# FoX attention head loop on one core: a finished pair's division and splits, the next pair's transposes, the rows of maxima and the probability copies

## The chip, the cores and the metric

One core of a Trainium2 chip runs the whole layer. The metric is device time in microseconds for one execution, as the median over several executions. TensorE (PE, with its weight loads as PEld), VectorE (DVE), ScalarE (ACT) and GpSimd (POOL) each work through their instructions in order; all DMAs of this kernel are issued from SyncE (SP), also in order.

## The reference

One encoder layer over 1024 frames of width 1024: a forgetting-attention group of 8 heads of 64 and an RG-LRU group, mixed by `w_out`, then a SwiGLU block. What the change touches is the attention:

```python
s = jnp.einsum('bhqd,bhkd->bhqk', qb, kb).astype(jnp.float32) * scale
s = s + (cum_logf[:, :, start:end, None] - cum_logf[:, :, None, :end])
s = jnp.where(mask[None, None], s, -jnp.inf)
p = jax.nn.softmax(s, axis=-1).astype(vb.dtype)
outs.append(jnp.einsum('bhqk,bhkd->bhqd', p, vb))
...
mixed = jnp.concatenate([rmsnorm(att, attn_out_g[l]), rmsnorm(rec, lru_out_g[l])], axis=-1)
x = x + mixed @ w_out[l]
```

All numbers are float32. The kernel keeps float32 accuracy on TensorE by splitting an operand into a rounded part and a rest (`split`: the rounded part is made on ACT, the rest on DVE), so that one product becomes three matmuls.

## The kernel before, in words

The heads are taken one after the other, `h` = 0 to 7; two heads make a pair `p`. A head has 12 steps (`att_steps`): four key blocks for the first half of the queries (512 of them), eight for the second half. A step makes scores transposed, keys by queries, in a PSUM bank `st` (3 of them): L676 multiplies one split part, L677 adds the rest together with two extra rows, the bias of the key and the row of maxima of the query, and L679 adds the causal mask on the diagonal. ACT takes the exponential into `pt` (L684, 3 buffers). The rounded copy `ringh` is made on ACT (L686) or on DVE (L688), in turn, the rest `ringl` on DVE (L689), in a ring of four. LAG[h] steps later PE multiplies them with the values into bank `o` (L698, three matmuls). Row 64 of the values is ones, so the denominators come out with the outputs; ACT copies both out (`oe`, L704), and SP takes them to `attr` and `dq`.

The row of maxima of a head is found one head ahead (`max_steps`): for each of eight query blocks `qb` PE makes plain scores in a bank `mx` (2 of them, L284, L286), DVE takes the maximum (L287, `nm`); `rows(half)` transposes four columns of them (`mt`, L296, also in an `mx` bank), ACT copies the row (`mr`, L298), and a DMA puts it into the score operands (`set`, L299). Before, `rows(0)` comes after block 3 and `rows(1)` after block 7.

Between the steps of a head other work is interleaved, a list `extra` of pieces at a pace set by RATE[h]: at even heads `prep` (the transposes of the next pair's q and k, L250, and their split into `kh`, `kl`, `qh`, `ql`), the DMAs of `load_max`, the eight `max_steps`, `vprep` (values of the next head: cast on ACT, rest on POOL, L650), and at heads 2, 4 and 6 `finish_pair` of the pair before it: `spread` takes reciprocals of the denominators on DVE (L731) and sends them through DRAM (`rd`) to a tile `rb` (L732, L735), POOL multiplies the whole `attr` by it (L719, 128x1024), then come the split (L75 on ACT, L76 on DVE), the square on ACT and the sum of squares on POOL (L725). At head 7 `finish_6` does the same for head 6, with L740 on POOL, and `load_wa` brings the eight pieces of `w_out` for the attention half, through two buffers. Besides, 32 units of the LRU half's output projection (`fl`, L783, 12 matmuls each, in the single bank `tr`, evicted on DVE at L785) fill the steps at a pace FILL[h].

The code is written in that order, and a scheduler of the tile framework orders each engine's instructions from it when the kernel is built, from its own estimates of durations. So a piece can land some instructions away from where it is written.

## Time and profile before

| | us |
|---|---|
| median of 3 runs | 1193.15 |
| lowest, highest | 1187.73, 1193.55 |
| the profiled execution, its time | 1189.54 |
| its span, first to last instruction | 1187.8 |
| its mean granted TensorE clock | 0.991 |
| attention loop in the trace, from the first L676 to the last L698 | 268 to 462 |

The profiled execution lies between the lowest and the median run. The loop that the change touches is a sixth of the span. In the rows further down, a busy time is the time in which the engine had work, an idle time carries the name of the instruction that ended it, and DVE also counts as busy while one of its instructions is held up inside its own duration.

### The profile page before, as it was taken

The numbers are of one execution on the slowest core, as the hardware profiler recorded it, in microseconds if no ns is written. First come the engines' busy times: TensorE is split into PE (matmuls) and PEld (weight loads), VectorE is DVE, ScalarE is ACT, GpSimd is POOL, SyncE is SP. The second block draws the span as 40 slices with busy tenths as digits, with TensorE's granted clock in tenths as the row PEclk, the third lists the DMA queues.
The fourth block names the chain that finished last, engine by engine and source line by source line (L and its number), as shares of the span: only waits on it lengthen the run. The fifth ranks groups of instructions, "written<-read, shape, count | busy, mean of one in ns | idle before, by whom it ended". The sixth has DMA issues, their size and how long they took to land.

```text
span 1187.8 us, 16586 instructions
## 1 busy us (share of the span) xinstructions
PE 1146.5 (97%) x6137; PEld 971.1 (82%) x6137; DVE 812.5 (68%) x1357; ACT 514.6 (43%) x931; POOL 228.4 (19%) x192
## 2 busy tenths in 40 slices
PE   8999999998999899999699898999999999999998
PEld 7988999996878777788478787888888888888887
DVE  6436858768787866776768766865545555769693
ACT  7427766326555554433233233333333334444442
POOL 1000010012010211027433333442424200000000
PEclk9999999999999999999889999999999999999999
DMA  6021111135665667540455646333122489842220
GB/s 249 19 55 52 38 37 37 30 72 126 169 151 144 165 161 207 168 153 21 169 201 205 255 164 237 133 114 107 54 89 73 140 289 340 289 154 98 92 86 36
DMA packets 94924, 159.71 MB, mean 134 GB/s; under 512 B 13105, under 2 KB 56217, under 8 KB 93434
## 3 DMA queue, kind: packets, MB, share of 16 engines
q1 hardware_dynamic: 94842, 158.65, 42.3%
q8 instruction: 48, 0.79, 0.3%
q14 instruction: 34, 0.28, 0.1%
HBM read 103.41 MB, written 38.63 MB: 120 GB/s over the span
## 4 chain that ended last, share of the span: by engine, by line
PE 70%; DVE 14%; DMA 9%; issue 3%; ACT 2%; POOL 1%; SPq 1%; DVEq 0%; POOLq 0%; ACTq 0%
PE P L1371 17%; PE Pu L936 10%; PE Pg L936 8%; DMA wd<-in_w_down_dram 4%; PE pag L361 4%; PE pbk L377 4%; PE pbv L377 4%; PE pax L361 4%; PE pbq L377 3%; PE o L698 3%; PE fl L783 3%; DVE wd L1025 3%; DMA td<-wd 2%; PE mx L284 1%; PE st L676 1%
## 5 line engine op out<-in xcount | busy, mean ns | idle before, releaser
L1118 ACT ACTIVATE g<-g 128x512 f32<-128x512 f32 x40 | 25.3, 632 | 106.1 <-DVE g L1117 105.7
L684 ACT ACTIVATE pt<-st 128x512 f32<-128x512 f32 (+1 forms) x96 | 47.9, 508 | 53.5 <-PE st L679 26.5
L1025 DVE TENSOR_TENSOR wd<-wd 128x512 f32<-128x512 f32 x44 | 43.6, 992 | 39.7 <-DMA wd<-in_w_down_dram 39.1
L689 DVE TENSOR_TENSOR ringl<-pt,ringh 128x512 fp32r<-128x512 f32 (+2 forms) x96 | 57.7, 615 | 7.2 <-ACT ringh L686 5.8
L287 DVE TENSOR_REDUCE nm<-mx 128x1 f32<-128x512 f32 (+2 forms) x96 | 51.2, 550 | 11.1 <-PE mx L286 6.9
L783 PE MATMUL fl<-worec,rech 128*128 128x256 f32 x256 | 53.3, 290 | 0.9 <-DVE ql L76 0.7
L783 PEld LDWEIGHTS fl<-worec,rech 128*128 128x128 f32 x256 | 42.6, 193 | 3.1 <-DVE ql L76 1.1
L1117 DVE TENSOR_TENSOR g<-pug,Pg 128x512 f32<-128x512 f32 x30 | 20.5, 684 | 27.4 <-PE Pg L936 18.8
L676 PE MATMUL st<-set 128*128 128x512 f32 (+1 forms) x96 | 35.5, 372 | 3.3 <-ACT pt L684 3.2
L698 PE MATMUL o<-ringh,vh 128*128 128x512 f32 (+1 forms) x96 | 37.8, 394 | 0.0
L698 PE MATMUL o<-ringl,vh 128*128 128x512 f32 (+1 forms) x96 | 35.0, 365 | 2.1 <-DVE ringl L689 2.1
L783 PE MATMUL fl<-worec,recl 128*128 128x256 f32 x128 | 36.5, 285 | 0.0
L480 POOL TENSOR_TENSOR sqR<-sqR,i 128x1024 f32<-128x1024 f32 x3 | 7.2, 2397 | 150.8 <-ACT i L479 150.8
L1115 DVE TENSOR_TENSOR g<-g,puu 128x512 f32<-128x512 f32 x40 | 35.2, 879 | 0.3
L698 PE MATMUL o<-ringh,vl 128*128 128x512 f32 (+1 forms) x96 | 34.3, 358 | 0.3 <-POOL vl L650 0.3
L650 POOL TENSOR_TENSOR vl<-vn,vh 128x256 fp32r<-128x256 f32 x16 | 12.3, 776 | 112.1 <-ACT vh L649 112.1
L1114 DVE TENSOR_TENSOR puu<-puu,Pu 128x512 f32<-128x512 f32 x30 | 20.4, 682 | 17.9 <-PE Pu L936 17.8
L1086 POOL TENSOR_TENSOR S1g<-graw,graw 128x512 f32<-128x512 f32 x10 | 14.6, 1463 | 80.2 <-DVE au12l L73 12.5
L435 DVE SCALAR_TENSOR_TENSOR xc<-xr,vcol,xc 128x1023 f32<-128x1023 f32 (+2 forms) x12 | 15.4, 1280 | 18.5 <-ACT xc L433 18.4
L686 ACT CAST ringh<-pt 128x512 fp32r<-128x512 f32 (+1 forms) x48 | 26.4, 549 | 1.6 <-PE o L698 0.8
L861 PE MATMUL wa<-wah,atth 128*128 128x512 f32 x64 | 26.0, 406 | 1.0 <-ACT wah L72 1.0
L1086 POOL TENSOR_TENSOR S1u<-uraw,uraw 128x512 f32<-128x512 f32 x10 | 12.9, 1287 | 72.6 <-DVE ag92l L73 9.3
(2185 smaller groups left out, 4081.2 us busy)
## 6 DMA issues: line engine op xcount, KB each, us to landing
graw<-in_w_gate_dram SPq DMA_DIRECT2D x22, 512.0 KB
uraw<-in_w_up_dram SPq DMA_DIRECT2D x22, 512.0 KB
wd<-in_w_down_dram SPq DMA_DIRECT2D x22, 512.0 KB
gd<-g SPq DMA_DIRECT2D x22, 512.0 KB
td<-wd SPq DMA_DIRECT2D x11, 1024.0 KB
xt<-in_x_dram SPq DMA_DIRECT2D x8, 512.0 KB
set<-qh SPq DMA_DIRECT2D x16, 256.0 KB
xp<-in_x_dram SPq DMA_DIRECT2D x32, 128.0 KB
```

What stands on the lines that cost most here:

```text
L287: dve.tensor_reduce(out=nm[:, ch * 8 + qb:ch * 8 + qb + 1], in_=ps[:, :nk], axis=AX.X, op=ALU.max, negate=True)
L361: pe.matmul(ps[g][:, :n], a, r, start=(kc == 0 and m == 0), stop=(kc == KC - 1 and m == 2))
L377: pe.matmul(ps[g][:, :n], a, r, start=(kc == 0 and m == 0), stop=(kc == KC - 1 and m == 2))
L676: pe.matmul(ps[:, off:], s[:, KA, j * P:(j + 1) * P], s[:, QA, qs:qs + N], start=True, stop=False)
L684: act.activation(out=pt[:, off:], in_=ps[:, off:], func=AF.Exp)
L689: dve.tensor_sub(out=pl[:, off:], in0=pt[:, off:], in1=f32(ph[:, off:]))
L698: pe.matmul(ot[:, off:], a[:, j * VW:j * VW + P], r[:, off:], start=(j == 0 and m == 0), stop=(j == jmax and m == 2))
L783: pe.matmul(ps[:, :256], a, r, start=(n == 0), stop=(n == 11))
L936: pe.matmul(ps, a[:, k, :], chunk(b, k), start=first and m == 0, stop=last and m == 11)
L1025: dve.tensor_sub(out=wd[:, o, :], in0=wd[:, a, :], in1=wd[:, b, :])
L1115: dve.tensor_mul(out=g, in0=g, in1=tmp)
L1371: pe.matmul(ps, x_[:, bs], y_, start=(begin and m == 0), stop=(end and m == 2))
```

## The change

- The pieces of a pair. `prep` becomes four pieces (k and q, two halves of 512 columns each) instead of one, `finish_pair` becomes seven (`start` with the reciprocals and the DMAs, then multiplication, split and square, two halves each). They are spread over the steps between the maxima by a new function `others`, in place of the tables VP and FIN.
- Engines. The multiplication by `rb` and the sum of squares go from POOL (1024 columns) to DVE (two times 512); `finish_6`'s multiplication too (one instruction). POOL keeps `vprep`.
- Rows of maxima. `rows(0)` comes after block 4, and `rows(1)` is the first piece of the next head, so one more piece stands between a half's last maximum and its transposition.
- Copies. Every fourth rounded copy of a probability tile stays on DVE, instead of every second; 24 of 96 go over to ACT, of 384 columns (two in each head) and 512 (one).
- Buffers and pace. `attr` gets two buffers, `rbl` its own tile, and RATE is 12 at heads 2, 4 and 7 as at head 1, and 11 at head 6.

```diff
@@ -238,18 +238,22 @@
     kn = [[None] * 2 for _ in range(2)]
     vn = [[None] * 2 for _ in range(2)]
 
-    def prep(p):
+    def prep_steps(p):
 
         c, cc = p // 2, (p % 2) * P
+        steps = []
         for nm, src, g, th, tl in (("k", kn, KG, "x0", "x1"), ("q", qn, QG, "x2", "x3")):
-            h = slot(th, f"{nm}h{p}", F32R)
-            l = slot(tl, f"{nm}l{p}", F32R)
-            for half in range(2):
+            def piece(half, nm=nm, src=src, g=g, th=th, tl=tl):
+                if half == 0:
+                    stage[nm + "h"] = slot(th, f"{nm}h{p}", F32R)
+                    stage[nm + "l"] = slot(tl, f"{nm}l{p}", F32R)
+                h, l = stage[nm + "h"], stage[nm + "l"]
                 ps = bank("st" if p == 0 and half else "tr", f"tr{p}{nm}{half}")
                 for b in range(4):
                     pe.transpose(ps[:, b * P:(b + 1) * P], src[c][half][:, b, cc:cc + P], ident)
                 split(ps, h[:, hs(half)], l[:, hs(half)], gain=col(g))
-            stage[nm + "h"], stage[nm + "l"] = h, l
+            steps += [lambda half=half, f=piece: f(half) for half in range(2)]
+        return steps
 
     kbs = [None] * 3
 
@@ -299,11 +303,8 @@
                 sp.dma_start(out=f32(s[64:65, QB, hs(half)]), in_=f32(mr))
             return step
 
-        for half in range(2):
-            for qb in range(4 * half, 4 * half + 4):
-                steps.append(mk_step(qb))
-            steps.append(rows(half))
-        return steps
+        m = [mk_step(qb) for qb in range(NB)]
+        return m[:5] + [rows(0)] + m[5:], rows(1)
 
     def sumsq_to_rstd(sq, dst, n, ps, b0=0, b1=NB):
         for b in range(b0, b1):
@@ -522,7 +523,8 @@
                 mid()
                 sumsq_to_rstd(sqR, rsR, AW, bank("tr", "ssR"))
                 proj_B(c, (4, 5), n, evac, ("st", "st", "o", "o"))
-                for s in max_steps(0):
+                first, last_row = max_steps(0)
+                for s in first + [last_row]:
                     s()
                 proj_B(c, (6, 7), n, evac, ("st", "st", "o", "o"))
             else:
@@ -594,7 +596,8 @@
             fes[0] = log_f()
         proj_vkq("k1", kn, evac_qk(1, kn, "k"), mid=f1)
         proj_vkq("q0", qn, evac_qk(0, qn, "q"), mid=log_f2)
-        prep(0)
+        for f in prep_steps(0):
+            f()
 
         def first_head():
             sets[0] = big("hA", "set0")
@@ -682,7 +685,7 @@
                 nring[0] += 1
                 ph, pl = ringh[:, i, :], ringl[:, i, :]
                 act.activation(out=pt[:, off:], in_=ps[:, off:], func=AF.Exp)
-                if nring[0] % 2:
+                if nring[0] % 4:
                     act.copy(out=ph[:, off:], in_=pt[:, off:])
                 else:
                     dve.tensor_copy(out=ph[:, off:], in_=pt[:, off:])
@@ -698,7 +701,7 @@
                     pe.matmul(ot[:, off:], a[:, j * VW:j * VW + P], r[:, off:], start=(j == 0 and m == 0), stop=(j == jmax and m == 2))
                 if j == jmax:
                     if o == 0 and half == 0:
-                        attr[p] = az.tile([P, S], F32, tag="attr", name=f"attr{p}")
+                        attr[p] = az.tile([P, S], F32, tag="attr", name=f"attr{p}", bufs=2)
                         dqs[p] = cp.tile([P, 4, 4], F32, tag="dq", name=f"dq{p}", bufs=2)
                     oe = az.tile([VW, 512], F32, tag="oe", name=f"oe{h}{half}", bufs=2)
                     act.copy(out=oe, in_=ot[:VW, :])
@@ -711,18 +714,30 @@
 
         return [mk_step(half, j) for half in range(2) for j in range(4 * half + 4)]
 
-    def finish_pair(p):
-        rb = spread(p, (0, 1))
+    def finish_steps(p):
+
         a = attr[p]
-        atth[p] = slot("q%d" % p, f"atth{p}", F32R)
-        attl[p] = slot("k%d" % p, f"attl{p}", F32R)
-        pool.tensor_mul(out=a, in0=a, in1=rb)
-        split(a, atth[p], attl[p], gain=col(Ag + p))
-        if p == 0:
-            act.activation(out=sqA, in_=a, func=AF.Square)
-        else:
-            act.activation(out=rb, in_=a, func=AF.Square)
-            pool.tensor_add(out=sqA, in0=sqA, in1=rb)
+        u = {}
+
+        def start():
+            u["rb"] = spread(p, (0, 1))
+            atth[p] = slot("q%d" % p, f"atth{p}", F32R)
+            attl[p] = slot("k%d" % p, f"attl{p}", F32R)
+
+        def scale(half):
+            dve.tensor_mul(out=a[:, hs(half)], in0=a[:, hs(half)], in1=u["rb"][:, hs(half)])
+
+        def parts(half):
+            split(a[:, hs(half)], atth[p][:, hs(half)], attl[p][:, hs(half)], gain=col(Ag + p))
+
+        def square(half):
+            if p == 0:
+                act.activation(out=sqA[:, hs(half)], in_=a[:, hs(half)], func=AF.Square)
+            else:
+                act.activation(out=u["rb"][:, hs(half)], in_=a[:, hs(half)], func=AF.Square)
+                dve.tensor_add(out=sqA[:, hs(half)], in0=sqA[:, hs(half)], in1=u["rb"][:, hs(half)])
+
+        return [start] + [lambda f=f, half=half: f(half) for f in (scale, parts, square) for half in range(2)]
 
     def spread(p, heads):
 
@@ -735,9 +750,13 @@
             sp.dma_start(out=rb[o * HD:(o + 1) * HD, :], in_=rd[2 * p + o:2 * p + o + 1, :].broadcast_to([HD, S]))
         return rb
 
-    def finish_6():
-        rb = spread(3, (0,))
-        pool.tensor_mul(out=attr[3][:HD, :], in0=attr[3][:HD, :], in1=rb[:HD, :])
+    rb6 = []
+
+    def finish_6a():
+        rb6.append(spread(3, (0,)))
+
+    def finish_6b():
+        dve.tensor_mul(out=attr[3][:HD, :], in0=attr[3][:HD, :], in1=rb6[0][:HD, :])
 
     def finish_half(half, oe):
 
@@ -755,10 +774,10 @@
             pe.matmul(ps[:HD, j * P:(j + 1) * P], rc[:, j:j + 1].broadcast_to([P, HD]), ident, start=True, stop=True)
         a = attr[3]
         dve.tensor_mul(out=a[HD:, hs(half)], in0=oe[:HD, :], in1=ps[:HD, :])
-        rb = az.tile([P, S], F32, tag="rb", name=f"rbl{half}")
+        rb = az.tile([P, 512], F32, tag="rbl", name=f"rbl{half}", bufs=1)
         split(a[:, hs(half)], atth[3][:, hs(half)], attl[3][:, hs(half)], gain=col(Ag + 3))
-        act.activation(out=rb[:, 512:], in_=a[:, hs(half)], func=AF.Square)
-        dve.tensor_add(out=sqA[:, hs(half)], in0=sqA[:, hs(half)], in1=rb[:, 512:])
+        act.activation(out=rb, in_=a[:, hs(half)], func=AF.Square)
+        dve.tensor_add(out=sqA[:, hs(half)], in0=sqA[:, hs(half)], in1=rb)
 
 
     wr_tile = [None, None]
@@ -793,9 +812,7 @@
 
     FILL = (4, 8, 4, 6, 6, 1, 3, 9)
     LAG = (3, 3, 2, 3, 2, 3, 3, 2)
-    RATE = (9, 12, 10, 10, 8, 9, 9, 12)
-    VP = (1, 3, 10, 6, 5, 6, 6, 1)
-    FIN = (3, 11, 10, 11, 8, 7, 3, 2)
+    RATE = (9, 12, 12, 10, 12, 9, 11, 12)
 
     woa = []
 
@@ -809,22 +826,35 @@
         sp.dma_start(out=raw, in_=w_out[0, kc * P:(kc + 1) * P, hs(half)])
         split(raw, h[:, hs(half)], l[:, hs(half)])
 
+    rest_row = []
+
+    def others(h):
+
+        row = [rest_row.pop()] if rest_row else []
+        if h == 7:
+            wa = [lambda kc=kc, half=half: load_wa(kc, half) for kc in range(4) for half in range(2)]
+            return row + [finish_6a] + wa[:1] + [finish_6b] + wa[1:]
+        m, last_row = max_steps(h + 1)
+        rest_row.append(last_row)
+        v = [lambda: vprep(h + 1)]
+        lm = [lambda: load_max(h + 2)] if h < 6 else []
+        pr = prep_steps(h // 2 + 1) if h % 2 == 0 and h < 6 else []
+        if h == 0:
+            return pr[:2] + v + pr[2:] + lm + m
+        if h % 2:
+            return row + lm + m[:3] + v + m[3:]
+        f = finish_steps(h // 2 - 1)
+        e = row + pr + lm + m[:1]
+        if h == 6:
+            e += m[1:3]
+            m = m[2:]
+        e += f[:1] + m[1:3] + v + m[3:4] + f[1:2] + m[4:5] + f[2:3] + m[5:6] + f[3:4]
+        return e + [x for y in zip(f[4:], m[6:]) for x in y] + f[4 + len(m[6:]):] + m[6 + len(f[4:]):]
+
     vprep(0)
     pend = []
     for h in range(H):
-        extra = []
-        if h % 2 == 0 and h + 2 < H:
-            extra.append(lambda: prep(h // 2 + 1))
-        if h + 2 < H:
-            extra.append(lambda: load_max(h + 2))
-        if h + 1 < H:
-            extra += max_steps(h + 1)
-            extra.insert(VP[h], lambda: vprep(h + 1))
-        if h >= 2 and h % 2 == 0:
-            extra.insert(FIN[h], lambda: finish_pair(h // 2 - 1))
-        if h == 7:
-            extra += [lambda kc=kc, half=half: load_wa(kc, half) for kc in range(4) for half in range(2)]
-            extra.insert(3, finish_6)
+        extra = others(h)
         steps = att_steps(h)
         ne = nf = 0
         for i, (sc, pv) in enumerate(steps):
```

How it moves instructions, at three places.

DVE, from the reciprocals of pair 2 (`dq`, at head 6) to the split of that pair; `ringl` are the rests of probability tiles of heads 6 and 7, `xp` evictions of fill units, `rb` is the tile that comes through DRAM. Before:

```order
L785 SCALAR_TENSOR_TENSOR xp_4952<-fl_4954,rsR,xp_4952 128x256
L688 CAST ringh<-pt_1_7_5098 128x256
L689 TENSOR_TENSOR ringl<-pt_1_7_5098,ringh 128x256
L689 TENSOR_TENSOR ringl<-pt_0_0_5187,ringh 128x512
L688 CAST ringh<-pt_0_1_5198 128x384
L689 TENSOR_TENSOR ringl<-pt_0_1_5198,ringh 128x384
L689 TENSOR_TENSOR ringl<-pt_0_2_5215,ringh 128x256
L688 CAST ringh<-pt_0_3_5234 128x256
L689 TENSOR_TENSOR ringl<-pt_0_3_5234,ringh 128x256
L785 SCALAR_TENSOR_TENSOR xp_5055<-fl_5057,rsR,xp_5055 128x256
L76 SCALAR_TENSOR_TENSOR attl_4915<-attr_4483,vcol,atth_4914 128x1024
L785 SCALAR_TENSOR_TENSOR xp_5105<-fl_5107,rsR,xp_5105 128x256
```

and now:

```order
L692 TENSOR_TENSOR ringl<-pt_1_3_5021,ringh 128x512
L692 TENSOR_TENSOR ringl<-pt_1_4_5041,ringh 128x512
L804 SCALAR_TENSOR_TENSOR xp_5050<-fl_5052,rsR,xp_5050 128x256
L692 TENSOR_TENSOR ringl<-pt_1_5_5071,ringh 128x384
L692 TENSOR_TENSOR ringl<-pt_1_6_5091,ringh 128x256
L691 CAST ringh<-pt_1_7_5106 128x256
L692 TENSOR_TENSOR ringl<-pt_1_7_5106,ringh 128x256
L728 TENSOR_TENSOR attr_4466<-attr_4466,rb_4932 128x512 x2
L804 SCALAR_TENSOR_TENSOR xp_5113<-fl_5115,rsR,xp_5113 128x256
L76 SCALAR_TENSOR_TENSOR attl_4936<-attr_4466,vcol,atth_4935 128x512 x2
L738 TENSOR_TENSOR sqA<-sqA,rb_4932 128x512 x2
L804 SCALAR_TENSOR_TENSOR xp_5130<-fl_5132,rsR,xp_5130 128x256
```

The multiplications (L728) and the sums of squares (L738) now stand in DVE's own order, in front of the evictions of the next two fill units and, behind them, of head 7's first rest; before, only the split's second half stood there, behind four rests of head 7.

SP at head 4, from the reciprocals' DMA (`rd`) on; `kh` is the next pair's rounded keys. Before:

```order
L732 DMA rd<-dq_3832 128x4x4
L261 DMA qms<-qh_4301 64x1024
L770 DMA wor_4595<-in_w_out_dram 128x2x256
L735 DMA rb_4456<-rd 64x1024
L786 DMA x1d<-xp_4317 128x256
L735 DMA rb_4456<-rd 64x1024
L786 DMA x1d<-xp_4375 128x256
L777 DMA xp_4427<-in_x_dram 128x256
L770 DMA wor_4599<-in_w_out_dram 128x2x256
```

and now:

```order
L747 DMA rd<-dq_3827 128x4x4
L711 DMA attr_4466<-oe_4468 64x512
L712 DMA dq_4467<-oe_4468 128x1x4
L796 DMA xp_4421<-in_x_dram 128x256
L750 DMA rb_4412<-rd 64x1024
L265 DMA set_2785<-kh_4317 64x1024
L750 DMA rb_4412<-rd 64x1024
L303 DMA set_2998<-mr_4526 1x4x128
L265 DMA qms<-qh_4348 64x1024
```

In both, one or two loads stand between the two halves of `rb`; now it is the one of `kh_4317`, which needs both transposes of the keys to be split, and the row `mr` of the next head's first half follows it.

PE at the beginning of head 3, where the second half's row of that head is transposed (`mt`), before among the last value products of head 2:

```order
L698 MATMUL o_1_3868<-ringh,vh_3016 128x384
L698 MATMUL o_1_3868<-ringh,vl_3017 128x384
L250 MATMUL tr2q_3684<-ident,qn_2662 128x128 x4
L296 MATMUL mt_3924<-ident,nm_3654 4x128
L698 MATMUL o_1_3868<-ringl,vh_3016 128x384
L676 MATMUL st_0_1_4005<-set_2998 128x384
L677 MATMUL st_0_1_4005<-set_2998,set_2785 128x384
L679 LDWEIGHTS identb
L679 MATMUL st_0_1_4005<-mk,identb 128x128
```

and, now, where the second half's scores take up that row (L680 is before's L677), with the maxima of head 4 (`mx`) in front:

```order
L288 MATMUL mx_4_0_4127<-set_2998,qms 128x512
L288 MATMUL mx_4_1_4130<-set_2998,qms 128x256
L290 LDWEIGHTS identb
L290 MATMUL mx_4_1_4130<-mq,identb 128x128
L300 MATMUL mt_4162<-ident,nm_3971 4x128
L288 MATMUL mx_5_0_4178<-set_2998,qms 128x512
L288 MATMUL mx_5_1_4181<-set_2998,qms 128x256
L290 LDWEIGHTS identb
L290 MATMUL mx_5_1_4181<-mq,identb 128x128
L680 MATMUL st_1_0_4072<-set_2998,set_2785 128x512
L680 MATMUL st_1_1_4099<-set_2998,set_2785 128x512
L680 MATMUL st_1_2_4113<-set_2998,set_2785 128x512
```

From the transposition of the row to its first use PE now has 65 instructions at this head (2314 to 2379 in its order), before 41 (2262 to 2303).

## Rows read from the trace of the kernel before

**Rows 1.** The page's part 1, busy time, share and instructions of each engine.

```profile
PE 1146.5 (97%) x6137; PEld 971.1 (82%) x6137; DVE 812.5 (68%) x1357; ACT 514.6 (43%) x931; POOL 228.4 (19%) x192
```

**Rows 2.** Stretches of the loop: span, busy times by engine, clock, DMA share, GB/s.

```profile
268.00:290.00 22.00, 18.53 (x101) 12.69 (x99) 19.55 (x43) 15.64 (x34) 7.62 (x16) 1.00 0.54 122
...
386.00:407.00 21.00, 17.45 (x119) 14.91 (x118) 17.09 (x29) 10.71 (x20) 5.46 (x3) 1.00 0.53 142
...
466.00:480.00 14.00, 12.31 (x53) 8.62 (x52) 11.49 (x25) 4.76 (x8) 2.39 (x1) 1.00 0.55 180
447.00:450.30 3.30, 3.30 (x14) 2.73 (x13) 3.27 (x5) 2.18 (x4) 1.14 (x1) 0.50 0.82 219
```

**Rows 3.** Timeline of PE: start, duration, instruction, in brackets idle time and releaser.

```profile
287.62 0.50 PE L698 MATMUL o<-ringl,vh 128*128 128x512 f32 x1 [1.15 <-DVE ringl L689]
...
351.83 0.27 PE L296 MATMUL mt<-ident,nm 128*4 128x128 f32 x1 [1.16 <-DVE nm L287]
...
400.89 0.27 PE L296 MATMUL mt<-ident,nm 128*4 128x128 f32 x1 [1.90 <-DVE nm L287]
...
446.05 0.50 PE L676 MATMUL st<-set 128*128 128x512 f32 x1 [2.46 <-ACT pt L684]
```

**Rows 4.** Timeline of POOL, multiplications and sums of squares.

```profile
347.24 2.93 POOL L719 TENSOR_TENSOR attr<-attr,rb 128x1024 f32<-128x1024 f32 x1 [4.58 <-DMA rb<-rd]
...
396.83 2.39 POOL L719 TENSOR_TENSOR attr<-attr,rb 128x1024 f32<-128x1024 f32 x1 [7.64 <-DMA rb<-rd]
401.43 2.39 POOL L725 TENSOR_TENSOR sqA<-sqA,rb 128x1024 f32<-128x1024 f32 x1 [2.21 <-ACT rb L724]
...
440.99 2.40 POOL L719 TENSOR_TENSOR attr<-attr,rb 128x1024 f32<-128x1024 f32 x1 [22.79 <-DMA rb<-rd]
445.66 2.47 POOL L725 TENSOR_TENSOR sqA<-sqA,rb 128x1024 f32<-128x1024 f32 x1 [2.27 <-ACT rb L724]
467.21 2.39 POOL L740 TENSOR_TENSOR attr<-attr,rb 64x1024 f32<-64x1024 f32 x1 [19.07 <-DMA rb<-rd]
```

**Rows 5.** Timeline of DVE at these times, and of ACT at 443.

```profile
348.62 2.09 DVE L689 TENSOR_TENSOR ringl<-pt,ringh 128x512 fp32r<-128x512 f32 x1 [0.72 <-ACT ringh L686]
...
396.86 2.91 DVE L689 TENSOR_TENSOR ringl<-pt,ringh 128x512 fp32r<-128x512 f32 x1 [0.99 <-ACT ringh L686]
...
402.08 2.82 DVE L76 SCALAR_TENSOR_TENSOR attl<-attr,vcol,atth 128x1024 fp32r<-128x1024 f32 x1
404.82 0.68 DVE L689 TENSOR_TENSOR ringl<-pt,ringh 128x512 fp32r<-128x512 f32 x1
...
443.43 1.15 ACT L75 ACTIVATE atth<-attr,vcol 128x1024 fp32r<-128x1024 f32 x1 [3.76 <-POOL attr L719]
444.61 1.28 DVE L76 SCALAR_TENSOR_TENSOR attl<-attr,vcol,atth 128x1024 fp32r<-128x1024 f32 x1 [3.01 <-ACT atth L75]
446.52 1.90 DVE L688 CAST ringh<-pt 128x512 fp32r<-128x512 f32 x1 [0.23 <-ACT pt L684]
```

**Rows 6.** Groups by line and shape in the loop: busy us, mean ns.

```profile
L287 DVE TENSOR_REDUCE nm<-mx 128x1 f32<-128x512 f32 x42 | 28.5, 682 | 5.5 <-PE mx L284 3.3 <-PE mx L286 2.1
...
L688 DVE CAST ringh<-pt 128x384 fp32r<-128x384 f32 x16 | 6.6, 413 | 3.5 <-ACT pt L684 3.2
...
L76 DVE SCALAR_TENSOR_TENSOR ql<-tr3q,vcol,qh 128x512 fp32r<-128x512 f32 x2 | 1.5, 748 | 1.3 <-ACT qh L75 1.3
...
L686 ACT CAST ringh<-pt 128x512 fp32r<-128x512 f32 x32 | 19.9, 621 | 0.6
```

**Rows 7.** Timeline of SP: the reciprocals' two DMAs of pair 1.

```profile
388.30 0.38 SPq L732 DMA_DIRECT2D rd<-dq  x1
...
391.08 0.47 SPq L735 DMA_DIRECT2D rb<-rd  x1
```

**Rows 8.** The chain that ended last, pieces on PE: a fill unit, a value product.

```profile
291.09 1.49 PE fl L783 x12
...
304.05 0.69 PE o L698 x3
```

## The prediction

> **What bounds the kernel now.** First the busy times: PE works in 97% of the span [rows 1], so only what makes PE wait, or slows its clock, can be won; a microsecond taken from DVE or ACT elsewhere is worth nothing. Then the stretches of the loop, 268 to 480 us: PE's idle time is the span less PE's busy time, and it sits in patches, 3.47 us in 268 to 290, 3.55 in 386 to 407 and 1.69 in 466 to 480 [rows 2]. Then PE's timeline, for what ended each patch [rows 3]: a rest of a probability tile (1.15 us, head 0), a maximum from DVE that the transposition `mt` needs (1.16 and 1.90), and an exponential on ACT (2.46). Last, the three other engines at those times, which name the cause. At 347, 397, 401 and 446 POOL has a tensor of 1024 columns in work [rows 4], and each time a DVE instruction lasts as long as POOL's does: a rest takes 2.09 and 2.91 us where it takes 0.68 at 404.8, the split 2.82 against 1.28, a cast of 512 columns 1.90 against 0.41 for 384 [rows 5, 6]. So DVE is held while POOL works, and the reductions queue behind it. [...]
>
> **POOL's five big operations go to DVE.** They leave behind 1.16 + 1.90 + 2.46 = 5.5 us of PE waits [rows 3] and 3.3 us at half clock, which cost 1.65 [rows 2]: 7.2 us in all. I take all of it as gained. On DVE the holds end, (2.09 - 0.68) + (2.91 - 0.68) + (2.82 - 1.28) + (1.90 - 0.41) = 6.7 us [rows 5, 6]. In their place come six half products and four half sums, each at the price of a rest, two SBUF operands of 512 columns, 0.68 us, so 6.8 us, and `finish_6`'s product of 1024 columns, twice that, 1.4. DVE has room for it: it is busy 17.1 of 21 us in the worst stretch, holds included [rows 2].
>
> **Copies.** 24 casts leave DVE, at 0.41 us each [rows 6] 9.9 us. On ACT they cost at most 24 times 0.62, the price of 512 columns, 14.9 us over eight heads; ACT is busy 10.7 of 21 us and 15.6 of 22 [rows 2], so they are hidden there. DVE's relief reaches PE only where DVE is full: 268 to 290, busy 19.55 of 22 [rows 2]. There head 0's three casts, 1.2 us, can take away the wait of 1.15 [rows 3]; the work that DVE still has there (a chain of small operations for q's norm) speaks for half. I take 0.6, between 0 and 1.15.
>
> **The next pair's pieces.** In 386 to 407 some 3.55 - 1.90 = 1.65 us of PE idle time are left beside the maximum [rows 2, 3], beside the split of q and k. Cutting it up takes no work away. I take 0.6, between 0 and 1.65.
>
> Halving costs: a split of 512 columns takes 0.748 us, twice that is 1.50 against 1.28 for 1024 [rows 5, 6], 0.22 more for each of eight more DVE instructions, 1.8 us, beside the relief above; so nothing on the path. [...]
>
> **The new wait.** Before, POOL waited for `rb`, the reciprocals that come back through DRAM, and nothing else stood in its queue. Now DVE does, in order. From the issue of `rd` to POOL's start pair 1 took 396.83 - 388.30 = 8.5 us [rows 4, 7]. By the order of the new kernel 17 DVE instructions stand between the reciprocal and the product at heads 2 and 4, at some 0.6 us about 10 us: enough. At head 6 there are 13, of at most 0.7 us, nearer 7 in all, so DVE stands there for 0 to 2.5 us. Behind it are the evictions of two fill units, which share one bank, and head 7's first rest; PE meets that within two fill units. I take 1.5, which is nearer to the upper end since SP puts a load and an `x1d` store in front of `rb`. [...]
>
> **Rows of maxima.** `rows(1)` moves to the head that uses it. Its chain is a transposition (0.27 [rows 3]), a copy on ACT, SP's queue and a small DMA, for which 391.08 - 388.30 = 2.8 us is the nearest row, since `rb` can't be issued before `rd` has landed [rows 7]. At head 3 PE now has 65 instructions between transposition and use, before 41, among them two fill units of 1.49 us and twelve value products of at most 0.23 [rows 8]: some 8 us. Before, with less, none of PE's waits is put down to this DMA. So 0 to 1 us a head if SP is held up; I take 0.5 in all. Another price is nearer: at head 5 the new order lines up seven chunks of maxima with little else for PE, two banks, and DVE needs up to 0.68 us for each [rows 6], some 4.3 us, in which PE has about 3 us of work. 1.3 us, between 0 and 3 over all heads.
>
> **The tail.** `finish_6`'s product was 2.39 us on POOL, at 467.2 after a wait of 19.07 for `rb` [rows 4]; on DVE it takes 1.4, behind all of head 7's rests. PE's 1.69 us after 466 [rows 2] hang on the last pieces of `w_out` as well, which come through two buffers as before. I take 0, from -1.7 to +3 (a DVE queue that holds the buffers a little longer).
>
> **Sum**, against the profiled execution: 1189.54 - 7.2 - 0.6 - 0.6 + 1.5 + 0.5 + 1.3 = 1184.4. That execution lies 3.6 below the median shown and 1.9 below the mean of the three runs; I expect the new median where such a mean is, 1186.
>
> **Rivals.**
> - All patches vanish. PE's idle time in the rows is 3.47 + 1.16 + 3.55 + 2.46 + 1.69 = 12.3, and 1.65 of clock: 1189.54 - 14 + 1.9 = 1177. For it: DVE ends with some 8 us less work than before (6.7 + 9.9 - 6.8 - 1.4). Against it: head 0's chain and the tail are not touched.
> - Given back. Where the new order puts the maxima in front of the second half's scores, DVE takes them first and the rests later, and PE waits for the rests at the end of the head, about 0.7 us, one rest, in each of seven heads: 4.9 more, 1191. For it: two banks and one DVE. Against: DVE has less to do than before.
> - Slower. DVE stands at the product with `rb` still under way, at all three pairs, since the second half of `rb` is now issued behind a load that needs the next pair's keys. Nothing in DVE's queue passes. A stop of 5 us each, and each time a half clock of 1.65 as after the wait at 446, makes 20 us in place of the 1.5: 1186.3 - 1.5 + 20 = 1205. It decides from (7.2 + 1.2) / 3 = 2.8 us a pair. For it: a landing took 8.5 us at a DMA share of 53% [rows 2, 4, 7], and the load in front of the second half can add to it. Against: 10 us of DVE work in front.
>
> **How the numbers follow.** About 0.5%, 6 us, is what a measurement of this kernel can tell from no change; against 1193.15 faster means below 1187.2. The forecast (1181 to 1191) has a chance of 0.52, of which 0.40 lie below 1187.2; all patches gone 0.12; given back 0.24; slower 0.12. So faster 0.52, same 0.36, slower 0.12. The range goes from the case with all patches gone to half the way into the slower one: 1175 to 1198.
>
> **What would show it.** Right: no DVE rest over 1 us in the loop, no PE wait over 1.5 us between 345 and 450, no half clock there, DVE at the product waiting for `rb` at head 6 only. Wrong: a wait of DVE for `rb` of over 3 us at heads 2 and 4, PE standing at L680 (before's L677) for the row's DMA, PE idle over 4 us after the last head, or a new stretch at half clock.

## The result, and the profile after

After: 1198.6 us, median of six executions (1196.9 to 1201.7). Before, on the same chip, 1191.8 (1187.7 to 1193.6). The ratio, worked out over all these executions, is 1.0071 (the two medians alone give 1.0058), interval 1.0052 to 1.0090: slower, where 1186 with 1175 to 1198 had been forecast. The profiled execution of after took 1201.7, its span is 1199.9.

Busy times, the line that answers to [rows 1]:

```profile
PE 1159.8 (97%) x6137; PEld 980.6 (82%) x6137; DVE 807.2 (67%) x1347; ACT 523.3 (44%) x961; POOL 213.7 (18%) x186
```

PE does the same 6137 matmuls and is busy 13.3 us longer, so the loss is in how long they take. The stretches of [rows 2] again, and between them those in which the clock fell (columns as there; the clock stands behind POOL's busy time):

```profile
268.00:290.00 22.00, 20.22 (x89) 14.51 (x88) 16.06 (x34) 14.96 (x34) 6.82 (x16) 0.77 0.43 98
273.20:283.30 10.10, 9.59 (x29) 7.25 (x29) 8.58 (x22) 5.66 (x11) 2.05 (x2) 0.50 0.60 140
361.90:365.20 3.30, 3.30 (x15) 3.11 (x15) 2.30 (x4) 2.15 (x5) 0.00 (x0) 0.50 0.44 111
386.00:407.00 21.00, 20.47 (x127) 16.47 (x127) 19.43 (x39) 15.87 (x34) 1.75 (x2) 1.00 0.60 149
416.50:423.30 6.80, 6.80 (x20) 4.59 (x19) 4.62 (x9) 4.72 (x10) 0.00 (x0) 0.50 0.27 61
447.00:450.30 3.30, 3.30 (x23) 2.85 (x21) 0.84 (x3) 0.95 (x2) 0.00 (x0) 1.00 0.98 300
466.00:480.00 14.00, 11.48 (x54) 9.32 (x52) 8.66 (x21) 6.59 (x14) 0.00 (x0) 0.80 0.69 231
474.60:484.70 10.10, 9.49 (x33) 7.91 (x34) 4.73 (x16) 2.83 (x6) 0.00 (x0) 0.50 0.15 52
```

The half clock at 447 is gone, and four other stretches have come, 30.3 us in the rows where the rows of before have 3.3. From the first scores of head 0 (268.1 in both) to the first transposition of the part that follows attention, `x2n`, before takes 216.4 us and after 229.7:

```profile
484.52 1.06 PE L973 MATMUL t<-ident,x2n 128*128 128x128 f32 x8
```

```profile
497.86 0.38 PE L1003 MATMUL t<-ident,x2n 128*128 128x128 f32 x2
```

(before and after, timelines of PE). The whole loss of this pair of executions lies there: 13.3 us, against 12.1 between the spans. 27.0 us more at half clock cost an estimated 13.5, half of their length, if all of PE's work is twice as slow there, and some 12 by the value products of 512 columns, which start 0.43 us apart in after at 421 (clock 0.50) and 0.23 at 289 (1.00; timeline of PE). PE's waits of that stretch, summed over its timeline, fell from 12.2 us to 9.6; among them those of [rows 3] at the transposition `mt`, 1.16 and 1.90, are now one of 0.59 (PE). DVE's rests, 2.09 and 2.91 in [rows 5], are short again: the longest in the loop takes 0.91 us, and after a product in halves three of them take 1.49 us together (DVE):

```profile
359.43 0.27 PE L300 MATMUL mt<-ident,nm 128*4 128x128 f32 x1 [0.59 <-DVE nm L291]
```

```profile
347.02 1.28 DVE L728 TENSOR_TENSOR attr<-attr,rb 128x512 f32<-128x512 f32 x2
...
351.80 1.49 DVE L692 TENSOR_TENSOR ringl<-pt,ringh 128x512 fp32r<-128x512 f32 x3
```

So what was to go has gone, and in this pair of executions the clock took back as much and more. The largest wait of PE in the few microseconds before each of the four falls, or across it, is 0.77, 0.59, 0.35 and 1.35 us: none is a stop like the 2.46 that stood before the fall at 447 [rows 3].

### The profile page after: what moved, and what is told of

Read it like the earlier page. It is cut to its first block, busy times and chain, and to the rows that moved or that the text cites. A ratio compares the mean times of both kernels' runs of the same rounds, so it can differ in the third digit from the quotient of the medians.

```text
span 1199.9 us, 16582 instructions
## 1 busy us (share of the span) xinstructions
PE 1159.8 (97%) x6137; PEld 980.6 (82%) x6137; DVE 807.2 (67%) x1347; ACT 523.3 (44%) x961; POOL 213.7 (18%) x186
## 4 chain that ended last, share of the span: by engine, by line
PE 72%; DVE 13%; DMA 9%; issue 2%; ACT 2%; POOL 1%; SPq 1%; DVEq 0%; POOLq 0%; ACTq 0%
PE P L1401 17%; PE Pu L966 10%; PE Pg L966 8%; DMA wd<-in_w_down_dram 4%; PE pag L362 4%; PE pbk L378 4%; PE pbv L378 4%; PE pax L362 4%; PE o L701 3%; PE pbq L378 3%; PE fl L802 3%; PE wa L891 3%; DVE wd L1055 3%; DMA td<-wd 2%; PE mx L288 2%
## 5 line engine op out<-in xcount | busy, mean ns | idle before, releaser
L692 DVE TENSOR_TENSOR ringl<-pt,ringh 128x512 fp32r<-128x512 f32 (+1 forms) x96 | 54.5, 588 | 11.3 <-ACT ringh L689 10.5
L679 PE MATMUL st<-set 128*128 128x512 f32 (+1 forms) x96 | 38.8, 404 | 0.9 <-ACT pt L687 0.9
L689 ACT CAST ringh<-pt 128x512 fp32r<-128x512 f32 (+2 forms) x72 | 38.1, 550 | 0.7
L81 POOL TENSOR_TENSOR rs<-rs,neghalf 128x1 f32<-128x1 f32 x16 | 9.8, 613 | 129.4 <-DVE rs L80 123.6
L288 PE MATMUL mx<-set,qms 67*128 67x512 f32 (+2 forms) x72 | 27.6, 401 | 1.4 <-ACT mr L302 0.7
```

The lines of the kernel that those rows point to most:

```text
L288: pe.matmul(ps[:, :w], qm[:67, qb * P:(qb + 1) * P], kb[:67, j0 * P:j0 * P + w], start=True, stop=not diag)
L692: dve.tensor_sub(out=pl[:, off:], in0=pt[:, off:], in1=f32(ph[:, off:]))
```

## Experiments

The ratios are against the kernel before, measured beside each kernel on the same chip.

### Is it the clock by itself?

Theory one: the thin places are to blame, and matmuls put there give the time back. Theory two: the clock only goes along with a loss in waits and order. `a_fill0` is after with five matmuls at head 0's start whose result is overwritten; by theory one the 10.1 us at half clock there go, by theory two only the matmuls' own time is added, five of 0.23 us by [rows 8]. `a_fill` is after with 25 at all four places (the edit of `a_fill0`; the 14 behind the last head stand elsewhere):

```
+  WARM = {(0, 0, 3): 2, (0, 1, 0): 3}
+  for _ in range(WARM.get((h, half, j), 0)):
+      pe.matmul(ps, s[:, KA, j*P:(j+1)*P], s[:, QA, half*512:half*512+512], start=True, stop=True)
   pe.matmul(ps[:, off:], s[:, KA, j*P:(j+1)*P], s[:, QA, qs:qs+N], start=True, stop=False)
```

> After, plus five matmuls of 512 columns whose result is overwritten, at the start of head 0 (two ahead of the scores of tile 3, three ahead of the first scores of the second half), where PE waited 0.73, 0.17 and 0.77 us and then ran at 0.50 from 273.13 to 283.37. [...] Theory two (the loss is in waits and in the order, the clock only goes along): the time stays at 1198.6 or rises by up to 1.1.

> After, plus such matmuls of 512 columns at every place where the clock fell in the loop of after: five at head 0's start, three at the start of the second half of head 3 (run of maxima, fall at 361.87), three in that of head 5 (fall at 416.49), and 14 behind the last value products, where PE waits for the last pieces of w_out (fall at 474.51). Theory one: up to 30.7 us at half clock go, up to 15 us of cost, for at most 5 us of matmuls of which some lie in waits: 1183 to 1191, so at or below the kernel before. If only half of the stretches go: 1190 to 1195. Theory two: 1199 to 1203.

Measured: 1.0090 (1.0065 to 1.0116) and 1.0093 (1.0072 to 1.0113), medians 1199.1 and 1200.2. The windows of `a_fill0`, head 0's start and then the whole stretch up to `x2n`:

```profile
268.00:290.00 22.00, 19.20 (x101) 13.86 (x99) 20.15 (x42) 16.17 (x34) 6.77 (x16) 1.00 0.56 128
268.00:490.20 222.20, 211.15 (x1242) 171.10 (x1241) 162.63 (x333) 121.47 (x260) 15.92 (x28) 0.97 0.61 157
```

Head 0 runs at full clock now, as theory one said, and yet the median stays: the clock falls at other places (0.97 over the stretch). That profiled execution took 1194.5 with a mean clock of 0.987; the slowest of the same kernel took 1203.1 with 0.983. The four executions of `a_fill` have mean clocks of 0.983 to 0.990 where after has 0.981 to 0.984, and the one at 0.990 still took 1200.0: a better clock alone doesn't bring the time back, though the 25 matmuls take a part of it themselves. Both medians lie where theory two put them. Theory one in this form has fallen; what makes the holes is to be looked for in the edits.

### One part at a time

The forecast's largest term alone: before, with POOL's five operations and `finish_6`'s product on DVE, whole and at their old places.

```
-  pool.tensor_mul(out=a, in0=a, in1=rb)
+  dve.tensor_mul(out=a, in0=a, in1=rb)
   (the sum of squares in finish_pair and the product in finish_6 alike)
```

> Before, with the five operations of 1024 columns on DVE instead of POOL, in one piece and at before's places; nothing else is changed. The prediction's term alone: 1191.8 - 7.2 + up to 1.5 = 1184.6 to 1186, with no DVE rest above 1 us and no half clock at 447 to 450. Rival (DVE stands at the product for rb with the rests behind it, since here no step is put between): PE waits of 2 to 5 us at each of three pairs, each with a new stretch at half clock: 1195 to 1205.

Measured: 0.9946 (0.9929 to 0.9962), 1183.2 against 1189.1: 5.8 us less, where the forecast's terms 7.2 and 1.5 make 5.7. Its DVE, around the products:

```profile
347.21 0.68 DVE L689 TENSOR_TENSOR ringl<-pt,ringh 128x512 fp32r<-128x512 f32 x1
347.81 1.22 DVE L719 TENSOR_TENSOR attr<-attr,rb 128x1024 f32<-128x1024 f32 x1
...
395.65 0.69 DVE L689 TENSOR_TENSOR ringl<-pt,ringh 128x512 fp32r<-128x512 f32 x1 [0.99 <-ACT ringh L686]
...
438.35 1.23 DVE L719 TENSOR_TENSOR attr<-attr,rb 128x1024 f32<-128x1024 f32 x1 [1.25 <-DMA rb<-rd]
```

The rests are back at 0.68, and DVE waits for `rb` at head 6, 1.25 us, and 1.48 at `finish_6`'s product. PE's waits up to `x2n` are 7.8 us, 4.4 less than before's 12.2. The half clock at 447 is gone, but one of the same length stands at 473.6:

```profile
473.60:477.00 3.40, 3.40 (x9) 2.64 (x8) 2.71 (x5) 1.15 (x2) 0.55 (x1) 0.50 0.81 312
```

Then the other parts, each on top of this kernel, and from the other side `a_rows`, after with the second row back in the same head for heads 0 to 5. The edits are shortened: in `d_prep` and `d_fin` the tables VP and FIN are shifted to fit, `d_fin` has two buffers of `attr`, and in `d_rows` `max_steps` is the one of after:

```
d_copy
-  if nring[0] % 2:
+  if nring[0] % 4:
d_prep
-  extra.append(lambda: prep(h // 2 + 1))
+  extra += prep_steps(h // 2 + 1)
d_fin
-  extra.insert(FIN[h], lambda: finish_pair(h // 2 - 1))
+  for k, f in enumerate(finish_steps(h // 2 - 1)):
+      extra.insert(FIN[h] + 2 * k, f)
d_rows
-  extra += max_steps(h + 1)
+  m, last_row = max_steps(h + 1)
+  extra += m
+  if rest_row: extra.insert(0, rest_row.pop())
+  rest_row.append(last_row)
a_rows
-  m, last_row = max_steps(h + 1); rest_row.append(last_row)
+  m, last_row = max_steps(h + 1)
+  if h < 6: m = m + [last_row]
+  else: rest_row.append(last_row)
```

> The kernel with the five operations on DVE (1183.2, ratio 0.9946), plus the copies alone: every fourth cast on DVE instead of every second. By the prediction's term: 0.6 less, ratio 0.994, same stretches at half clock. If the copies are what made the clock fall at head 0 (ACT then has exponential and cast in a row for each of the first tiles): half clock at 273 to 283, 5.1 us more, ratio 0.999.

> The kernel with the five operations on DVE, plus the next pair's transposes and splits in four pieces over the steps, alone. By the prediction's term: 0.6 less, between 0 and 1.65, ratio 0.993 to 0.9946. If the pieces are what costs (the bank of the transposes is shared with the fill units, so that each piece makes a fill unit wait and the other way round): PE waits of over 1 us at the pieces and the fill units, ratio 0.997 to 1.002.

> The kernel with the five operations on DVE, plus the division, the split and the square of a finished pair in halves over the steps, alone. By the prediction: the halves cost 1.8 us of DVE off the path, ratio 0.9946 within 0.002. If the halves are what costs: ratio 0.998 or more, with PE waits at exponentials or rests at heads 2, 4 and 6.

> The kernel with the five operations on DVE, plus the rows of maxima alone: the first row behind the fifth block, the second at the start of the head that uses it. By the prediction's terms 0.5 + 1.3 = 1.8 more, ratio 0.996. By undoing it in after (1.0071 became 1.0028): 4 to 6 us more, ratio 0.998 to 1.000, with new stretches at half clock in the loop. If the rows cost only together with the other parts: 0.9946.

> After, with the second row of maxima back at the end of the same head's maxima (heads 0 to 5; head 7's row stays at the start of head 7). The rows as a cause of their own (a copy and a small DMA nearer to their use, seven chunks lined up ahead of the scores that need the row): the time falls by 2 to 5 us, with no half clock at 416 to 423. If the rows only move the thin places about: other stretches at half clock in other places, time within 3 us of 1198.6, and the span less half of the half-clock time stays within 2 us of after's.

Measured: `d_copy` 0.9929 (0.9907 to 0.9952), `d_prep` 0.9947 (0.9928 to 0.9965), `d_fin` 0.9919 (0.9892 to 0.9946): none is seen to cost anything, and that the first and the last gain is not certain (for `d_fin` 0.9946 within 0.002 was expected). `d_rows` 1.0074 (1.0048 to 1.0099), 15 us over the kernel without it: more than either expectation had. `a_rows` 1.0028 (1.0012 to 1.0044): undoing six of the rows gives some 5 us back, and the half clock at 416 is gone. So the rows lose what the rest of the change wins, and more.

### Which of the two rows

```
   m = [mk_step(qb) for qb in range(NB)]
   return m[:5] + [rows(0)] + m[5:] + [rows(1)]       d_row0: the first row alone
   return m[:4] + [rows(0)] + m[4:], rows(1)          d_row1: the second alone, at the next head's start
```

`a_rows2` is after with both rows where before has them.

> The kernel with the five operations on DVE (ratio 0.9946), plus half of what the rows do: the first row of maxima behind the fifth block instead of the fourth; the second stays at the end of the same head's maxima. With both halves it was 1.0074. If the moved second row is the cause: 0.9946 within 0.002, no new half clock in the loop. If the first row is: above 1.003.

> The same kernel, plus the other half: the second row at the start of the head that uses it, the first behind the fourth block. If the moved second row is the cause: 1.004 to 1.008, 10 to 16 us over the kernel without it, with 10 to 14 us at half clock in the loop. If the first row is: 0.9946 within 0.002.

> After, with both rows of maxima where before has them, at all heads (the division of head 6 stands two pieces later so that its sums are there). If the rows are the whole loss: after (1.0071) falls to what the other parts give alone, 0.992 to 0.996, 1181 to 1186, with at most 4 us at half clock before the first head's output is done. If the earlier undoing of the second row at six heads (1.0028) was all that can be had: 1.001 to 1.004, and another part of after costs some 8 us that no part shows alone.

Measured: `d_row0` 0.9948 (0.9924 to 0.9972), nothing; `d_row1` 1.0079 (1.0050 to 1.0107), all of it; `a_rows2` 0.9990 (0.9967 to 1.0012), 9.6 us less than after and still some 5 above `b_dve`: between its two expectations. The stretch from the first scores to `x2n`, `b_dve` and then `d_row1`:

```profile
268.00:480.50 212.50, 203.81 (x1244) 166.10 (x1243) 166.60 (x349) 113.01 (x233) 15.72 (x28) 0.99 0.65 167
```

```profile
268.00:500.70 232.70, 218.17 (x1246) 175.52 (x1245) 168.96 (x349) 113.28 (x233) 16.38 (x28) 0.93 0.60 153
```

20.2 us longer in the profiled executions. The granted clock has 27 us more at 0.50 (five stretches of 30.1 us in `d_row1`, one of 3.4 in `b_dve`), an estimated 13.5 of cost; PE's idle time by these lines is 5.8 us more (14.5 against 8.7).

### Why the second row costs

What happens is seen at head 3 of `d_row1` (L674 and L675 are the two matmuls of a score tile; the second needs the row). Its PE:

```profile
351.20 0.27 PE L296 MATMUL mt<-ident,nm 128*4 128x128 f32 x1
...
353.92 0.40 PE L674 MATMUL st<-set 128*128 128x512 f32 x1
...
356.60 0.40 PE L674 MATMUL st<-set 128*128 128x512 f32 x1
...
359.30 0.40 PE L674 MATMUL st<-set 128*128 128x512 f32 x1
...
367.09 0.94 PE L675 MATMUL st<-set,set 67*128 67x512 f32 x3
```

and its SP:

```profile
356.65 0.34 SPq L784 DMA_DIRECT2D x1d<-xp  x1
...
360.83 0.33 SPq L784 DMA_DIRECT2D x1d<-xp  x1
361.20 0.46 SPq L269 DMA_DIRECT2D set<-qh  x1
362.98 0.46 SPq L706 DMA_DIRECT2D attr<-oe  x1
363.50 0.66 SPq L299 DMA_DIRECT2D set<-mr  x1
```

The row is transposed at 351.20; SP issues its DMA at 363.50, 12.3 us later, behind stores (`x1d`, `attr`) that wait for DVE and loads that wait for their turn. SP's waits for DVE from 350 to 367 make 7.3 of it (us in all, times, longest; the name is that of the DVE instruction that ended the wait):

```profile
SPq L784 <- DVE ringh L686: 2.3, 1, 2.3
SPq L784 <- DVE xp L783: 2.1, 1, 2.1
...
SPq L784 <- DVE nm L287: 1.6, 1, 1.6
SPq L706 <- DVE attl L76: 1.3, 1, 1.3
```

Meanwhile three score tiles are half done, at 353.92, 356.60 and 359.30, and hold the three `st` banks; their second matmuls come at 367.09, all three at once. ACT's last exponential before that starts at 352.90 and the next at 367.66; DVE's last rest starts at 354.62, PE's last value product at 359.77. From then on PE has a fill unit and maxima at DVE's pace. The same in after at head 5 (L679 and L680 are the two matmuls there), on PE

```profile
403.36 0.49 PE L679 MATMUL st<-set 128*128 128x512 f32 x1
405.10 0.27 PE L300 MATMUL mt<-ident,nm 128*4 128x128 f32 x1
...
412.55 0.50 PE L288 MATMUL mx<-set,qms 67*128 67x512 f32 x1
413.39 0.38 PE L288 MATMUL mx<-set,qms 67*128 67x256 f32 x1 [0.35 <-ACT mr L302]
...
415.12 0.96 PE L288 MATMUL mx<-set,qms 67*128 67x512 f32 x2 [0.23 <-DVE nm L291]
415.92 0.23 PE L290 MATMUL mx<-mq,identb 128*128 128x128 bf16 x1
415.96 1.17 PE L680 MATMUL st<-set,kb 67*128 67x512 f32 x3
```

and on SP, DVE and ACT:

```profile
409.52 0.33 SPq L805 DMA_DIRECT2D x1d<-xp  x1
409.90 0.47 SPq L273 DMA_DIRECT2D set<-qh  x1
410.46 0.66 SPq L303 DMA_DIRECT2D set<-mr  x1
```

```profile
413.09 3.86 DVE L291 TENSOR_REDUCE nm<-mx 128x1 f32<-128x512 f32 x6 [0.59 <-PE mx L288]
```

```profile
416.47 1.08 ACT L687 ACTIVATE pt<-st 128x512 f32<-128x512 f32 x2 [3.13 <-PE st L680]
```

12.6 us from the first half of a score to its second half, and at 416.5 the clock falls. PE shows next to no waits there, because in its order the maxima stand ahead of the scores; over the eight heads the two matmuls of the first score tile of the second half stand 80 places apart in before's order of PE, all eight added up, 323 in after's, 372 in that of `d_row1` (orders as the traces show them). In time the eight distances come to 12.1, 51.3 and 60.7 us. From the second row's transposition to the issue of its DMA after takes 5.3 to 9.7 us at each of heads 1 to 7.

Theory: SP's queue. Rival: the later transposition by itself. One line takes the DMA out of that queue, in `d_row1` (`d_row1_act`), in after (`a_act`), and in `b_dve` as a control (`d_act`):

```
-  sp.dma_start(out=f32(s[64:65, QB, hs(half)]), in_=f32(mr))
+  act.dma_start(out=f32(s[64:65, QB, hs(half)]), in_=f32(mr))
```

> The five operations on DVE and the moved second row (1.0079), with the rows' small DMAs issued by ACT, behind its own copy, instead of SP. If it is SP's queue that makes the row late: the issue follows the copy within 1 us, the second half's scores follow at once, half clock in the loop is at most 7 us, and the ratio is 0.994 to 0.998. If the later transposition itself costs: above 1.004.

> After, with the rows' small DMAs issued by ACT. If SP's queue is the cause of the rows' cost: as with the rows undone, 0.997 to 1.001, 1188 to 1192. If the later transposition itself costs: 1.005 to 1.009.

> The control: the five operations on DVE (0.9946), rows where before has them, their DMAs issued by ACT. If early rows are never waited for: 0.9946 within 0.002. If ACT's issue holds up exponentials: above 0.997. Below 0.992 if before too loses to SP's queue.

Measured: `d_row1_act` 0.9932 (0.9907 to 0.9958) instead of 1.0079; `a_act` 0.9960 (0.9941 to 0.9980) instead of 1.0071; `d_act` 0.9924 (0.9898 to 0.9950), by its interval no different from `b_dve`, though its 2.6 us less may be a gain of ACT's issue by itself; `d_row1_act` and `a_act` came out lower than expected, and of the signs one failed: `d_row1_act` has 10.2 us at half clock in its loop, not 7. Head 3 of `d_row1_act`, PE and ACT's queue:

```profile
340.40 0.27 PE L296 MATMUL mt<-ident,nm 128*4 128x128 f32 x1
...
341.00 0.58 ACTq L299 DMA_DIRECT2D set<-mr  x1
...
343.56 0.39 PE L674 MATMUL st<-set 128*128 128x512 f32 x1
345.86 0.48 PE L675 MATMUL st<-set,set 67*128 67x512 f32 x1
```

0.6 us from transposition to issue, 2.3 from the first half of the score to the second; 60 places and 10.2 us over all heads (173 and 27.1 in `a_act`). The stretch up to `x2n` in `a_act`:

```profile
268.00:477.20 209.20, 199.70 (x1235) 163.82 (x1234) 161.56 (x333) 123.97 (x260) 14.78 (x27) 0.99 0.65 168
```

The transposition is as late as in after (at head 5 3.9 us behind the first half of the first score, 1.7 in after), the clock is back at 0.99, and the change as it stands, with that one line, is faster than before. The rival falls. Not separated: PE's order changes together with the queue, and an early issue under after's order wasn't tried. In after and `d_row1` PE never stands at a second half's first L680 or L675, so the row has landed when PE gets there, and it is the order that holds the score back at that moment. But another order could have won little: at head 2 of `d_row1_act` PE does wait for the row, and the DMA takes 4.0 us from issue to use,

```profile
318.35 0.58 ACTq L299 DMA_DIRECT2D set<-mr  x1
...
322.36 0.50 PE L675 MATMUL st<-set,kb 67*128 67x512 f32 x1 [0.53 <-DMA set<-mr]
```

while in after the score follows SP's issue by 3.5 to 5.5 us at six of the seven heads 1 to 7 and by 8.8 at head 6, in `d_row1` by 3.6 us at head 3. With the issue so late, the score could hardly have come earlier.

Moving 16 small DMAs to ACT took 1.1% off after (1.0071 to 0.9960): the row's DMA had stood in line behind DMAs that wait, 5.4 and 12.3 us from transposition to issue at the two heads shown, 0.6 from ACT.

### What else after loses, and the best kernel

`a_rows2_rate` is `a_rows2` with before's pace of the steps at heads 2 and 4 (`RATE` 10 and 8 for 12 and 12). `best` is `d_fin` with `d_copy`, `fin_act` is `d_fin` with the rows' DMAs on ACT.

> After with the rows undone (0.999), and the pace of the steps at heads 2 and 4 as in before (10 and 8 for 12 and 12). If the slower pace is what the rest hangs on: 0.992 to 0.995. If it is the place of the pieces at head 0, where the half clock of this kernel lies: 0.998 to 1.000, with the same stretches at 275 to 295.

> Before, with the five operations on DVE, the finished pair's work in halves over the steps and every fourth cast on DVE; rows of maxima and the next pair's pieces as before. If the parts' gains add up (0.9946, then 0.9973 for the halves and 0.9983 for the casts): 0.990, 1178. If they hang on the same waits: 0.992, the better of the two alone.

> Before, with the five operations on DVE, the finished pair's work in halves over the steps, and the rows' DMAs issued by ACT. If the gains add up (0.9946; halves 0.9973 of that, ACT's issue 0.9978 of that): 0.990, 1179. If both take away the same waits: 0.992 within 0.002.

Measured: `a_rows2_rate` 0.9963 (0.9946 to 0.9980), so some of what stays may be the pace; the intervals overlap, the value lies between the two expectations, and the rest is open. `best` 0.9929 (0.9906 to 0.9953), no better than either part: the gains don't add up. `fin_act` 0.9909 (0.9885 to 0.9934), 1180.5 against 1190.7, the lowest of all, by its interval not apart from `d_fin`; it beats both kernels of the case.

## Why the prediction was wrong

- **POOL's operations to DVE** (-7.2, and +1.5 for the new wait): right in place; the size, 5.8 us by `b_dve` for the forecast's 5.7, is in part luck. In its trace PE's waits up to `x2n` fell by 4.4 us, but 3.4 us at half clock stayed, at another place, so the 1.65 for the clock didn't come there; that stretch is 3.8 us shorter, and the rest of the gain lies behind it. The hold by POOL shows in the rests, 2.09 and 2.91 us beside POOL [rows 5], 0.68 without it in `b_dve`; what holds them is not shown. The 2.46 of the forecast came by way of ACT, which stood 3.76 us at `atth` for POOL's product [rows 5]; in `b_dve` PE's waits for an exponential from 340 to 450 come to 0.2 us.
- **Copies, pieces, halves** (-0.6, -0.6, nothing on the path): not contradicted: the intervals of their runs, some 2 us to either side, hold the forecast, and they hold zero too; of the halves it was, if anything, too careful.
- **Rows of maxima** (0.5, and 1.3 for the runs): the step that failed. Alone the moved second row costs 15.8 us (0.9946 to 1.0079), in after 9.6 to 13 by `a_rows2` and `a_act`. Two readings went wrong. The chain behind the transposition was priced by the nearest row, 2.8 us between two DMAs of SP, "0 to 1 us a head if SP is held up"; it took 5.4 us to the issue at after's head 5 and 12.3 in `d_row1`, since SP's queue at that place is full of DMAs that wait. Before's own trace had a nearer row, at head 4:

```profile
361.99 0.27 PE L296 MATMUL mt<-ident,nm 128*4 128x128 f32 x1
...
368.64 0.66 SPq L299 DMA_DIRECT2D set<-mr  x1
```

There the queue took 6.6 us as well, but ahead of the first score that needs the row. And the 65 instructions between transposition and use were read as cover. They were the hole: other work that stands between the two halves of a score, while all three score banks are taken and no exponential can start. The 1.3 named the right place, the run of maxima at head 5, but as a little idle time of PE; what stands there is 12.6 us in which no score is finished.
- **What would show it**: DVE stands once before a product at heads 2 to 6, 2.4 us (put down to the load of `xp`; the product reads only `attr` and `rb`, so it is one of theirs), and 1.5 us for `rb` behind head 7; no DVE rest over 1 us, no PE wait over 1.5 between 345 and 450: nearly as put there. But "no half clock there" failed: 447 is clear, while the falls at 361.9 and 416.5 lie between 345 and 450, and they are the new stretches that were named as a sign of being wrong. PE standing at L680 for the row's DMA doesn't show either, though the row is the cause: maxima stand in front in PE's order, so the wait has no row of its own; the distance of two matmuls of one score tells it.
- **The clock**: the sum gave back 1.65 for the old stretch and had no term for new ones, though "a new stretch at half clock" stood under what would show it wrong. 27 us more of it, an estimated 13.5 us, is as large as the whole loss in the profiled pair. It isn't a cause by itself: in `d_rows`, 15 us slower than `b_dve`, 13.7 us more at half clock make only some 6.8 of it (the mean clocks of the profiled executions are 0.987 and 0.991), and PE's waits are 5.8 us more.
- **The rivals**: the slower one had DVE standing for `rb`; in after DVE stands before a product twice, 2.4 and 1.5 us. The engine held in order was SP, not DVE. "Given back" named maxima in front of the second half's scores, which is where PE's time went, but priced it at a rest in each head, 4.9 us. No rival had the row late in SP's queue.
- **The tail** (0, up to +3): head 7 up to `x2n` takes 49.0 us for 50.3 before, with 10.1 of them at half clock against 3.3.

## What to carry to other kernels

What follows is drawn from this one kernel. When a step moves, follow its DMA through the queue that issues it: what stands ahead there, and what those wait for, is its latency (12.3 us at head 3 of `d_row1`), not the time between two neighbours elsewhere (2.8 us [rows 7]). Instructions between a producer and its use are cover only if they keep the engines behind them fed; look at what holds the buffers meanwhile: at head 5 of after no score was finished for 12.6 us. A small DMA that others wait for belongs in a queue where nothing in front of it waits: from ACT the row's DMA was issued 0.6 us behind the transposition, from SP 5.4 and 12.3.

## What the runs showed of the hardware

In after the clock fell without a long stop of PE. From 403 to the fall at 416.5, from 1.00 to 0.50, PE's largest wait was 0.35 us; it ran fill units, and then maxima at DVE's pace (six reductions in 3.86 us). And the same kernel runs at different mean clocks: the five of `fin_act` took 1176.4 and 1177.0 at mean clocks of 0.994 and 0.993, and 1182.6 and 1183.0 at 0.988 and 0.987, with 1180.5 at 0.991 between them. Head 0's start, where after fell to 0.50, is one of the places where it can differ: in the profiled execution of `fin_act`, which leaves the rows where before has them, value products of 512 columns take 0.63 us at 281 and 0.39 at 285, so the clock was low there too. In that of `a_act`, which has the rows where after has them, it was 1.00 from 268 to 290. So not all of after's 30 us at half clock can be laid to the rows; 10.1 of them are at head 0 and 10.1 behind the last head's values.
